# Token-major u, v and q in groups of 512 weight columns, one bank per token tile, row tiles outermost

## The chip, the cores and the metric

The kernel runs on one core of one Trainium2 chip. The metric is the device time of one execution in microseconds: the median of three runs. A profiled execution, taken separately, gives the trace.

## What is computed

Two layers of a hybrid backbone over 512 latent tokens (x) and 256 context tokens (ctx), 1024 features, all in fp32. A layer begins with

```python
hx = modulate(rms_norm(x, norm1_g[l]), sx1, cx1)
hc = modulate(rms_norm(ctx, norm1_g[l]), sc1, cc1)
zx = split_in(hx @ w_in[l])   # a, b (conv) | q | k | v | u, v (gating) | 3 gates
```

and the parts of that product feed a convolution module (width 31, with a layer norm), a windowed attention with 8 query and 2 key heads, and a spatial gating unit (`gelu(u) * (sgu_w @ layer_norm(gelu(v)))`). Three gated projections are summed, projected and added to x; a gated MLP with a width-3 convolution follows. Layer 0 computes all this for x and ctx, layer 1 for x alone (and k, v of ctx).

## The kernel before, in words

Every product is exact to about fp32: activations and weights are split into a hi and a lo half, and three matmuls (hi hi, lo hi, hi lo) are accumulated. Weights come in raw tiles of 1 MB (tag `raw`, two buffers, SyncE's queue); `hilo` makes two halves of half a raw tile (one copy on ScalarE, line 114, one subtraction on VectorE, line 117; tag `hl`). Pairs of halves alternate between two pools: two pairs in `wp` and, from the spatial gating to the end of q, one pair in the pool of the gating stage.

Most products are feature-major (`linear_steps`): a weight tile of 128 columns is stationary, 512 x tokens or 256 ctx tokens move. Those of u, v, q and of k, v are token-major (`token_group`): 128 tokens are stationary, 256 weight columns move. A group of 256 columns is done one token tile after the other, 8 row tiles x 3 matmuls each; two token tiles share a bank. u, v and q have 512 columns each, so two groups; layer 0 has six token tiles (four of x, two of ctx), layer 1 four. Evacuations are a gelu on ScalarE (`uv_group`) or a copy (q).

PSUM has eight banks: tag `S` is one buffer of two banks, `b` has three, `x` two, `c` one. `acc_ps(0)` gives a bank for x, `acc_ps(1)` for ctx; where `wide[0]` is set, the first goes round x, x, b, b, b and the second round S, c, by a counter that only grows. `wide[0]` is set from the convolution's products to the end of u, and in the MLP, and not set for q.

The order of the code in a layer: convolution products a, b (`ab`); v, u, with background steps (`tick`: convolution taps on VectorE) between; gates of branch 0 with the spatial gating (`sgu`) in the background; k, v product (line 757); norm and rotation of k, its transposes (line 793, tag S); `drain` of the background; `conv_ln`, the layer norm of the convolution, with a mean matmul (line 570, tag S), and for x and for ctx the sums of squares (line 400, tag b) and their broadcast (line 413, tag b); q (line 807); two early gates of branch 2; then the projections of the convolution (tag cy as operand) and of the gating as filling between the steps of the attention.

Within that, instructions are planned by a list scheduler: each engine takes the first one in priority (the order of the code, shifted for weights and evacuations) whose inputs and buffers are there in the scheduler's own timing, and executes that order as it stands.

At the start of the MLP (`up_first`) four products per part of 256 tokens follow the sums and the broadcast of the norm of the parts, with the same tags.

Of the kernel before, what the change touches and what calls it, by code (L numbers as in the profile page):

```python
# [12 lines left out]
AF = mybir.ActivationFunctionType  # L13
# [43 lines left out]
def layout(inputs):  # L57
    """the arrays of the launch: transposes and concatenations of the inputs, by tiles of 128 partitions"""
    v = {k: np.asarray(a) for k, a in inputs.items()}
# [20 lines left out]
def body(tc, I, out):  # L80
# [19 lines left out]
    def acc_ps(c):  # L100
        """a bank for a product of x (0) or of ctx (1); where nothing else needs them, from the other tags too"""
        if not wide[0]:
            return c_ps() if c else x_ps()
        turns[c] += 1
        if c:
            return (c_ps, s_ps)[turns[1] % 2]()
        return (x_ps, x_ps, b_ps, b_ps, b_ps)[turns[0] % 5]()
# [27 lines left out]
    def newton(src, n, scale, tag):  # L135
        """1/sqrt(src*scale + EPS) of a [128, n] operand"""
        v = T(cp, [128, n], F32, "nv" + tag[0], 1)
        ts(v, src, float(scale), mul, EPS, add)
        t = T(cp, [128, n], I32, "nt" + tag[0], 1)
        ts(t, v.bitcast(I32), 1, ALU.logical_shift_right)  # L140
        y = T(cp, [128, n], I32, "ny" + tag, 1)
        ts(y, t, -1.0, mul, float(0x5F3759DF), add)
        ts(v, v, -0.5, mul)
        u = T(cp, [128, n], F32, "nu" + tag[0], 1)
        yf = y.bitcast(F32)
        for _ in range(3):
            tt(u, yf, yf, mul)
            tt(u, u, v, mul)
            stt(yf, u, 1.5, yf, add, mul)
        return yf  # L150

# [1 line left out]
    def evac():  # L153
# [55 lines left out]

# [1 line left out]
    msk = T(sp, [128, NT], F32, "t", NTP)[:, :512]  # L211
# [12 lines left out]

    # feature vectors of both layers, one column per 128 features
    def load_fv(l):
# [6 lines left out]
    def load_ff(l, pool):  # L233
        """taps and biases of the MLP's convolution, one column per 128 features"""
        ff = T(pool, [128, FF_N], F32, "ff", 1)
        nc.scalar.dma_start(out=ff, in_=I["ff"][l])
        return ff
# [41 lines left out]
    def load_cond():  # L279
        """silu(c), silu(c_ctx): hi and lo parts as columns, and rows in DRAM"""  # L280
        st = T(xp_, [128, 16], F32, "st", 1)
# [13 lines left out]
    def ada_start():  # L295
        """shift and scale of the first norm, both conditions; those of the first four feature tiles come first"""
        for g2 in range(2):
# [29 lines left out]
    def ada(l, pool, blocks, both):  # L327
        """modulations of 128 features each, by rows of the transposed matrix; of c_ctx too for those in both"""
        for h in range(2):
# [17 lines left out]

# [1 line left out]
    bgs = []  # L349
# [24 lines left out]
    def paced(r):  # L374
        """in the schedule, not before the products traced so far"""
        if last[0] is not None:
            tc.add_manual_dep(r.ins, last[0].ins.name, SCHED)

# [1 line left out]
    def segs_of(full):  # L380
# [14 lines left out]
    def rstd_diag(acc, o, n, scale):  # L395
        """1/sqrt of the feature sums of acc[:, o:o+n], by token tiles on the diagonals of [128, 128] blocks"""
        nt = n // 128
# [9 lines left out]
    def bcast_diag(dg, n, bp=None):  # L407
        """the diagonals on every partition"""
        if bp is None:
# [14 lines left out]
    def norm_mod(xs, bp, hs, o, n, a, sh):  # L424
        """hi and lo pages of x * bp * a + sh"""
        v = slice(o, o + n)
# [11 lines left out]
    def linear_steps(res, w, cs, hs, segs, k0=0):  # L438
        """feature-major product of one 128-column tile, w hi/lo [128, k, cols]: per segment (psum, offset, length, segment);
        yields the time that the tensor engine has been given"""  # L440
        nk = w[0].shape[1]
# [16 lines left out]
    def token_group(hs, c0, nt):  # L458
        """token-major product of a group of 256 columns: (psum [128, 2, 256], first of its two token tiles)"""
        raw = load8(I["w_in"][l], c0)  # L460
# [15 lines left out]

    def tg_parts(p, t0, ng):
        """parts of a pair of token tiles that lie in one tile of ng: (psum, group, index, count)"""
        if t0 // ng == (t0 + 1) // ng:
            return [(p, t0 // ng, t0 % ng, 2)]  # L480
        return [(p[:, a:a + 1], (t0 + a) // ng, (t0 + a) % ng, 1) for a in range(2)]

    def tr(o, i):
        nc.tensor.transpose(o, i, ident)

# [1 line left out]
    def load_x(gap=None):  # L487
# [32 lines left out]
    for l in range(2):  # L520
# [15 lines left out]

# [1 line left out]
        wide[0] = True  # L538
# [92 lines left out]

# [1 line left out]
        EVP[0] = 150  # L633
# [12 lines left out]

        def uv_group(dst, c0, c):
            for p, t0 in token_group(hs, c0 + c * 256, nt):
                for q, g, a, n in tg_parts(p, t0, ng):
                    with evac():  # L650
                        act(out=dst[g][:, a:a + n, c * 256:c * 256 + 256], in_=q, func=AF.Gelu_apprx_tanh)

        U = [page("g2", 4, n=1536).rearrange("p (t d) -> p t d", t=3) for _ in tg]
        Vv = [page("g2", 4, n=1536).rearrange("p (t d) -> p t d", t=3) for _ in tg]
        for c in range(2):
            uv_group(Vv, 2304, c)
            tick(11)

# [48 lines left out]
        ys = []  # L707
        for c in range(2):
            uv_group(U, 1792, c)
            tick(11)  # L710
        wide[0] = False

# [1 line left out]
        def gate_steps(b, j, dst):  # L714
# [14 lines left out]
        def gated_steps(dst, w, j, ys, ao=False):  # L729
            """projection of a branch, times (tanh + 1) of its gate in place: twice the sigmoid's share"""  # L730
            if j % 4 == 0:
# [20 lines left out]

# [1 line left out]
        vt = page("g2", 4, F32R, 1536)  # L754
# [8 lines left out]
        def head_norm(pg, tmp, ss):  # L763
            """sums of squares by head of pg [128, tiles, heads, 64]"""
            act(out=tmp, in_=pg.rearrange("p t h d -> p (t h) d"), func=AF.Square)
            V.tensor_reduce(out=ss, in_=tmp, axis=AX.X, op=add)

        def head_rot(pg, nh, tb, t0, n, sw, rs):
            """pg [128, n tiles, nh heads, 64] in place: scale by head, gain, rotation of the x tiles"""
            fl = pg.rearrange("p t h d -> p (t h) d")  # L770
# [34 lines left out]

# [1 line left out]
        Q = [T(sp, [128, 1536], F32, "g2", 4).rearrange("p (t i k d) -> p t i k d", t=3, i=4, k=2) for _ in tg]  # L807
        for g in range(2):
            for p, t0 in token_group(hs, 1024 + g * 256, nt):
                for q, gr, a, n in tg_parts(p, t0, ng):  # L810
                    with evac():
                        acopy(Q[gr][:, a:a + n, :, g, :], q.rearrange("p t (i d) -> p t i d", i=4))
        rings.pop()
# [25 lines left out]
        def fill(us):  # L839
            """dense products for that many microseconds of the tensor engine, in front of what is emitted next"""  # L840
            credit[0] = min(credit[0], 0) + us
# [7 lines left out]

        # pairs of heads of one token tile  # L850
        ssq = T(cp, [128, 48], F32, "ssq", 1)
# [32 lines left out]
        def keys_of(t):  # L884
            """key tiles, their runs in psum (offset, length, first key), offset of the mask"""
            if t < 3:
# [7 lines left out]
        def scores(pr, i):  # L894
            """probabilities of one head"""
            t, kv, i0, (qd, ql) = pr["t"], pr["kv"], pr["i0"], pr["q"]
# [23 lines left out]
        def turn_P(pr, g):  # L920
            """hi and lo parts of the transposed probabilities of two key tiles"""
            kk = keys_of(pr["t"])[0][g * 2:g * 2 + 2]
# [104 lines left out]
        wide[0] = True  # L1027
# [1 line left out]
        if l == 0:  # L1029
# [51 lines left out]

# [1 line left out]
        if l == 0:  # L1083
# [36 lines left out]
        def up_first(due):  # L1120
            """two pairs of tiles part by part, behind the norm of each part"""
            ws = [up_load(j) for j in range(2)]
# [96 lines left out]
```

## Time and profile before

| what | value |
|---|---|
| median of 3 runs | 2134.9 us (2134.14 to 2138.05) |
| profiled execution, span | 2133.2 us |
| TensorE matmul busy | 2098.5 us (98%) |
| weight loads (beside matmuls) | 1801.1 us (84%) |
| VectorE busy | 1569.4 us (74%) |
| ScalarE busy | 895.9 us (42%) |
| mean DMA rate | 99 GB/s |

A matmul's duration in the trace is from its start to its modelled end, and the next one starts before that, so what a matmul costs is the distance of starts. Groups below are named by line (L446), engine, operation and output tile <- input tiles, then the shapes.

### The profile page before, as it was taken

How to read it: one execution, taken by the hardware profiler on the slowest of the kernel's cores; microseconds unless marked ns; L12 is line 12 of the kernel's file. 1: busy time of each engine (PE TensorE's matmuls, PEld its weight loads, DVE VectorE, ACT ScalarE, POOL GpSimd, SP SyncE). 2: the span in 40 equal slices, each digit the busy share in tenths (PEclk: the TensorE clock that was granted, in tenths of full speed). 3: DMA queues.
4: the chain of work that ended last, by engine and by line, in shares of the span. 5: the costliest groups of instructions: out<-in, count | busy, mean ns of one | idle time of the engine just before them, and what ended most of it. 6: DMA issues, size and time to landing. Idle time of an engine off the chain costs nothing.

```text
span 2133.2 us, 30441 instructions
## 1 busy us (share of the span) xinstructions
PE 2098.5 (98%) x12108; PEld 1801.1 (84%) x12108; DVE 1569.4 (74%) x3134; ACT 895.9 (42%) x1489; POOL 0.2 (0%) x4
## 2 busy tenths in 40 slices
PE   6999999999999999999999999999999999999999
PEld 2899898877888998888888898979777888888887
DVE  6679887888757778867595767998877367655554
ACT  6522235567623453323231334434577336333331
POOL 0000000000000000000000000000000000000000
PEclk8999999999999999999999999999999999999999
DMA  8122112212245223444243423222111333232321
GB/s 274 60 76 66 53 60 80 89 50 80 79 111 184 76 83 135 141 137 148 99 149 103 164 75 105 88 76 80 60 40 60 91 129 99 94 104 79 119 91 67
DMA packets 158805, 210.94 MB, mean 99 GB/s; under 512 B 6724, under 2 KB 109892, under 8 KB 158664
## 3 DMA queue, kind: packets, MB, share of 16 engines
q1 hardware_dynamic: 154048, 202.40, 28.7%
q10 hardware_dynamic: 4616, 6.61, 1.0%
q8 instruction: 95, 1.56, 0.3%
q14 instruction: 46, 0.38, 0.1%
HBM read 204.78 MB, written 4.20 MB: 98 GB/s over the span
## 4 chain that ended last, share of the span: by engine, by line
PE 81%; DVE 11%; DMA 3%; ACT 3%; issue 1%; SPq 0%; DVEq 0%; ACTq 0%
PE x L446 10%; PE x L448 10%; PE x L447 10%; PE b L447 8%; PE b L446 8%; PE b L448 8%; DVE cy L120 4%; PE c L446 3%; PE c L447 3%; PE c L448 3%; PE S L907 2%; DVE hl L117 2%; PE b L944 2%; PE b L927 2%; PE S L446 2%; PE S L447 2%
## 5 line engine op out<-in xcount | busy, mean ns | idle before, releaser
L114 ACT ACTIVATE hl<-raw 128x1024 fp32r<-128x1024 f32 x264 | 279.0, 1059 | 487.3 <-PE c L447 199.0
L117 DVE TENSOR_TENSOR hl<-raw,hl 128x1024 fp32r<-128x1024 f32 x264 | 322.4, 1223 | 193.7 <-ACT hl L114 190.8
L446 PE MATMUL x<-h,hl 128*128 128x512 f32 (+1 forms) x760 | 294.3, 389 | 7.0 <-ACT h L114 7.0
L448 PE MATMUL x<-h,hl 128*128 128x512 f32 (+1 forms) x760 | 292.0, 385 | 1.6 <-DVE hl L117 1.6
L447 PE MATMUL x<-h,hl 128*128 128x512 f32 (+1 forms) x760 | 293.0, 386 | 0.0
L120 DVE SCALAR_TENSOR_TENSOR cy<-cy,fv 128x497 f32<-128x497 f32 (+29 forms) x240 | 208.3, 881 | 2.9
L447 PE MATMUL b<-h,hl 128*128 128x512 f32 (+1 forms) x552 | 203.6, 370 | 0.0
L446 PE MATMUL b<-h,hl 128*128 128x512 f32 (+1 forms) x552 | 203.5, 370 | 0.0
L448 PE MATMUL b<-h,hl 128*128 128x512 f32 (+1 forms) x552 | 202.9, 368 | 0.3 <-DVE hl L117 0.3
L446 PEld LDWEIGHTS x<-h,hl 128*128 128x128 f32 x760 | 145.0, 192 | 33.7 <-ACT h L114 7.9
L448 PEld LDWEIGHTS x<-h,hl 128*128 128x128 f32 x760 | 145.0, 191 | 28.7 <-DVE hl L117 2.7
L447 PEld LDWEIGHTS x<-h,hl 128*128 128x128 f32 x760 | 145.1, 191 | 24.2 <-DVE h L117 0.2
L448 PEld LDWEIGHTS b<-h,hl 128*128 128x128 f32 x552 | 103.9, 188 | 18.0 <-DVE hl L117 0.7
L446 PEld LDWEIGHTS b<-h,hl 128*128 128x128 f32 x552 | 103.9, 189 | 17.0
L447 PEld LDWEIGHTS b<-h,hl 128*128 128x128 f32 x552 | 104.0, 189 | 16.4
L446 PE MATMUL c<-h,hl 128*128 128x256 f32 x400 | 112.7, 282 | 0.1
L448 PE MATMUL c<-h,hl 128*128 128x256 f32 x400 | 112.7, 282 | 0.0
L447 PE MATMUL c<-h,hl 128*128 128x256 f32 x400 | 112.6, 281 | 0.1
L120 DVE SCALAR_TENSOR_TENSOR m<-b,ff,m 128x511 f32<-128x511 f32 (+2 forms) x118 | 80.9, 688 | 36.5 <-ACT m L1092 35.0
L339 DVE CUSTOM_DVE_ANT_0 t<-t,srow,adab 128x512 f32<-128x512 f32 (+1 forms) x128 | 92.4, 745 | 4.5 <-DMA t<-in_adat 4.2
L339 DVE CUSTOM_DVE_ANT_0 t<-t,srow,mod 128x512 f32<-128x512 f32 (+1 forms) x128 | 91.7, 746 | 1.8 <-DMA t<-in_adat 0.9
L114 ACT ACTIVATE PT<-b 128x512 fp32r<-128x512 f32 (+2 forms) x128 | 62.3, 500 | 58.6 <-PE b L944 39.6
(322 smaller groups left out, 5124.5 us busy)
## 6 DMA issues: line engine op xcount, KB each, us to landing
raw<-in_w_in SPq DMA_DIRECT2D x44, 1024.0 KB, 5.1
raw<-in_ffn_up SPq DMA_DIRECT2D x44, 1024.0 KB, 5.1
t<-in_adat SPq DMA_DIRECT2D x160, 256.0 KB, 3.0
raw<-in_ffn_down SPq DMA_DIRECT2D x22, 1024.0 KB, 4.9
raw<-in_w_o SPq DMA_DIRECT2D x8, 1024.0 KB, 7.1
g<-in_xt SPq DMA_DIRECT2D x8, 768.0 KB, 5.7
m<-in_ada SPq DMA_DIRECT2D x16, 256.0 KB, 5.4
h<-in_ada SPq DMA_DIRECT2D x16, 256.0 KB, 5.4
```

Of the source, the lines that this page charges most:

```text
L114: act(out=o, in_=i, func=AF.Copy)
L117: V.tensor_tensor(out=o, in0=a, in1=b, op=op)
L120: return V.scalar_tensor_tensor(out=o, in0=a, scalar=s, in1=b, op0=op0, op1=op1)
L339: paced(V.tensor_tensor_reduce(out=w[:, 512:].bitcast(BF16) if c else w[:, :512], in0=w[:, :512], in1=sr[:, c], scale=1.0, scalar=o if h e ...
L446: nc.tensor.matmul(p, w[0][:, k, cs], hi[:, o:o + n], start=(k == 0), stop=False)
L447: nc.tensor.matmul(p, w[0][:, k, cs], lo[:, o:o + n], start=False, stop=False)
L448: last[0] = nc.tensor.matmul(p, w[1][:, k, cs], hi[:, o:o + n], start=False, stop=(k == nk - 1))
L907: nc.tensor.matmul(sp_[:, o:o + n], ql[r, c], KT[kv][r, ko:ko + n], start=False, stop=True)
L927: r_ = nc.tensor.transpose(pt[:, a * 256 + i * 128:a * 256 + i * 128 + 128], pr["P"][i][:, (g * 2 + a) * 128:(g * 2 + a) * 128 + 128], ident)
L944: r_ = nc.tensor.matmul(po[:, :256], vs, half[:, a * 256:a * 256 + 256], start=fi and i == 0, stop=la and i == 1)
```

## The change

`token_wide` takes the place of `token_group` for u, v and q (k, v keep it). It takes one bank of 512 columns per token tile, all at once, and goes over the weights in four passes of two row tiles; in a pass every token tile gets its 6 matmuls of 512 columns. A raw load is now 512 rows by 512 columns, and `hilo` splits two row tiles by 512 columns. Evacuations are one per token tile, after the last pass. Of the 22 background steps of u or v 5 come after each of the first three passes and 7 at the end (before, 11 after each group). For q `wide[0]` is set. Docstrings and comments go too; they change nothing.

```diff
+    def token_wide(hs, c0, nt, between=None):
+        ps_ = [acc_ps(t >= 4)[:, :512] for t in range(nt)]
+        for q in range(4):
+            if q % 2 == 0:
+                raw = load4(I["w_in"][l], q * 256, c0).rearrange("p (k c) -> p k c", k=4)
+            w = hilo(raw[:, q % 2 * 2:q % 2 * 2 + 2, :], 2)
+            for t in range(nt):
+                for k in range(2):
+                    hi, lo = hs[q * 2 + k]
+                    c = slice(t * 128, t * 128 + 128)
+                    nc.tensor.matmul(ps_[t], hi[:, c], w[0][:, k, :], start=(q + k == 0), stop=False)
+                    nc.tensor.matmul(ps_[t], lo[:, c], w[0][:, k, :], start=False, stop=False)
+                    last[0] = nc.tensor.matmul(ps_[t], hi[:, c], w[1][:, k, :], start=False, stop=(q * 2 + k == 7))
+            if between and q < 3:
+                between()
+        return ps_
...
-        def uv_group(dst, c0, c):
-            for p, t0 in token_group(hs, c0 + c * 256, nt):
-                for q, g, a, n in tg_parts(p, t0, ng):
-                    with evac():
-                        act(out=dst[g][:, a:a + n, c * 256:c * 256 + 256], in_=q, func=AF.Gelu_apprx_tanh)
+        def uv_group(dst, c0):
+            for t, p in enumerate(token_wide(hs, c0, nt, lambda: tick(5))):
+                with evac():
+                    act(out=dst[t // ng][:, t % ng, :], in_=p, func=AF.Gelu_apprx_tanh)
+            tick(7)
...
-        for c in range(2):
-            uv_group(Vv, 2304, c)
-            tick(11)
+        uv_group(Vv, 2304)
...
-        for c in range(2):
-            uv_group(U, 1792, c)
-            tick(11)
+        uv_group(U, 1792)
...
-        for g in range(2):
-            for p, t0 in token_group(hs, 1024 + g * 256, nt):
-                for q, gr, a, n in tg_parts(p, t0, ng):
-                    with evac():
-                        acopy(Q[gr][:, a:a + n, :, g, :], q.rearrange("p t (i d) -> p t i d", i=4))
+        wide[0] = True
+        for t, p in enumerate(token_wide(hs, 1024, nt)):
+            with evac():
+                acopy(Q[t // ng][:, t % ng].rearrange("p i k d -> p k i d"), p.rearrange("p (k i d) -> p k i d", k=2, i=4))
+        wide[0] = False
```

## Rows read from the trace of the kernel before

**Rows 1.** The page, part 1: busy time, share of the span and instructions of each engine.
```profile
PE 2098.5 (98%) x12108; PEld 1801.1 (84%) x12108; DVE 1569.4 (74%) x3134; ACT 895.9 (42%) x1489; POOL 0.2 (0%) x4
```

**Rows 2.** Timeline of TensorE, layer 0's v: start us, us, what; 48 starts apart.
```profile
121.38 0.28 PE L471 MATMUL x<-hl,h 128*128 128x256 f32 x1
...
127.14 0.28 PE L471 MATMUL b<-hl,h 128*128 128x256 f32 x1
```

**Rows 3.** Timeline of TensorE, gates of layer 0, 512 columns; 15 starts apart.
```profile
241.21 0.39 PE L446 MATMUL x<-h,hl 128*128 128x512 f32 x1
...
244.61 0.39 PE L446 MATMUL x<-h,hl 128*128 128x512 f32 x1
```

**Rows 4.** Busy time by stretch: v, u of layer 0; v, u, then gates of layer 1.
```profile
core 0: us, PE busy (x) PEld busy (x) DVE busy (x) ACT busy (x) POOL busy (x), PEclk, DMA share, GB/s
121.00:191.00 70.00, 69.95 (x580) 69.52 (x579) 61.09 (x87) 19.20 (x29) 0.00 (x0) 1.00 0.15 46
...
1334.00:1382.00 48.00, 47.32 (x388) 46.84 (x387) 45.99 (x95) 21.97 (x34) 0.00 (x0) 1.00 0.27 89
1382.00:1439.00 57.00, 54.44 (x261) 44.47 (x260) 56.12 (x91) 17.86 (x25) 0.00 (x0) 0.97 0.23 74
```

**Rows 5.** Timeline of TensorE, layer 0, from q's first matmul to the convolution's projection.
```profile
284.80 0.28 PE L471 MATMUL x<-hl,h 128*128 128x256 f32 x1
...
296.13 0.88 PE L484 MATMUL S<-identr,t 128*128 128x128 f32 x6 [0.20 <-DVE t L117]
...
300.90 1.53 PE L570 MATMUL S<-t,ones 128*128 128x512 f32 x4
...
321.69 0.60 PE L413 MATMUL b<-t,ones 128*128 128x256 f32 x2
...
325.23 0.40 PE L446 MATMUL x<-h,hl 128*128 128x512 f32 x1
...
341.90 0.39 PE L446 MATMUL x<-cy,hl 128*128 128x512 f32 x1
```

**Rows 6.** Timeline of VectorE: last readers of mean and broadcast, last convolution operand.
```profile
307.21 0.42 DVE L120 SCALAR_TENSOR_TENSOR cy<-S,cy 128x256 f32<-128x256 f32 x1
...
324.86 1.01 DVE L117 TENSOR_TENSOR t<-cy,b 128x512 f32<-128x512 f32 x2
...
333.16 0.96 DVE L117 TENSOR_TENSOR cy<-t,cy 128x768 fp32r<-128x768 f32 x1
```

**Rows 7.** Timeline of layer 1's same stage, TensorE, and the broadcast's last reader on VectorE.
```profile
1456.35 0.28 PE L471 MATMUL x<-hl,h 128*128 128x256 f32 x1
...
1482.70 1.12 PE L413 MATMUL b<-t,ones 128*128 128x512 f32 x2 [0.19 <-DVE t L117]
...
1484.13 0.40 PE L446 MATMUL x<-h,hl 128*128 128x512 f32 x1
...
1495.06 0.40 PE L446 MATMUL x<-cy,hl 128*128 128x512 f32 x1
...
1488.62 0.68 DVE L117 TENSOR_TENSOR t<-cy,b 128x512 f32<-128x512 f32 x1
```

**Rows 8.** The page, part 5: weight splits (busy us, mean ns, idle before).
```profile
L114 ACT ACTIVATE hl<-raw 128x1024 fp32r<-128x1024 f32 x264 | 279.0, 1059 | 487.3 <-PE c L447 199.0
L117 DVE TENSOR_TENSOR hl<-raw,hl 128x1024 fp32r<-128x1024 f32 x264 | 322.4, 1223 | 193.7 <-ACT hl L114 190.8
```

**Rows 9.** Timeline of TensorE, start of the MLP in layer 0.
```profile
730.30 0.28 PE L448 MATMUL x<-h,hl 128*128 128x256 f32 x1
732.61 0.70 PE L413 MATMUL b<-t,ones 128*128 128x256 f32 x2 [2.02 <-DVE t L117]
734.95 0.58 PE L446 MATMUL x<-h,hl 128*128 128x256 f32 x1 [1.65 <-ACT h L114]
...
741.93 0.50 PE L400 MATMUL b<-ones,t 128*128 128x1 f32 x4
742.29 0.36 PE L446 MATMUL b<-h,hl 128*128 128x256 f32 x1
```

**Rows 10.** Busy time and granted clock (PEclk) in the stretch after that idle time.
```profile
735.00:740.00 5.00, 5.00 (x23) 5.00 (x24) 4.25 (x12) 4.55 (x11) 0.00 (x0) 0.50 0.01 2
```

More of the change, by code (lines that the diff above doesn't have):

```diff
@@ L475, in token_group @@
         return res
[L477 to L481, printed above, removed]
+    def token_wide(hs, c0, nt, between=None):
[14 more added lines that the diff above has]
+        return ps_
     def tr(o, i):
```

## The prediction

> **What bounds the kernel now.** I read the busy table first: TensorE is occupied 98% of the span [rows 1], so the question is how densely it is fed. Start to start in the timeline, the 48 matmuls of 256 columns of one v tile take 5.76 us, 120 ns each [rows 2], and 15 matmuls of 512 columns take 3.40 us, 226.7 ns each [rows 3]. Then the table by stretch: in layer 0's v and u products TensorE has no hole (69.95 of 70 us) while VectorE has 9 us to spare; in layer 1 the same stage and the gate products behind it leave VectorE 2.0 us of 48 and 0.9 us of 57 [rows 4]. So layer 0's v and u are bound by TensorE's cadence, layer 1's by VectorE (31 convolution taps a channel tile, weight splits, gating). Last I read the stage from the k, v product to the convolution's projection, where two things run side by side: q's matmuls, and the chain k transposes, mean, deviation sums, broadcasts, on which the projection depends [rows 5 to 7]. There q is what keeps TensorE busy while that chain waits for VectorE and ScalarE.
>
> **Part 1, fewer and longer matmuls.** u, v and q take 3 products x 6 token tiles x 8 row tiles x 3 passes x 2 halves = 864 matmuls of 256 columns in layer 0 and 576 in layer 1; after the change 432 and 288 of 512. One long one for two short ones saves 240 - 226.7 = 13.3 ns [rows 2, 3]: 5.7 us in layer 0 (v and u 3.8, q 1.9) and 3.8 us in layer 1 (v and u 2.6, q 1.3), 9.6 us at most. Layer 0's v and u should keep their 3.8 us; in layer 1 I take 0.5 of 2.6, since VectorE has nothing to give there [rows 4] (bounds 0 and 2.6). q's share is inside part 3.
> The Trainium skill ("TensorE: Matmul & The Clock Gate", section "Back-to-back issue gap") gives columns / 2.4 GHz plus 2.5 ns for a gap; by that estimate a pair would save 2.5 ns, and all of them 1.8 us. The rows show a fixed part of some 13 ns per matmul, and the rows decide.
>
> **Part 2, weights.** A pass over two row tiles now uses one pair of halves: 36 matmuls x 226.7 = 8.2 us in layer 0, 24 x 226.7 = 5.4 us in layer 1. The next pair costs 1.06 us on ScalarE and 1.22 us on VectorE [rows 8], and three pairs are in the rings, so loading and splitting hide behind a pass. If the cover goes (the fourth pair shares a buffer with the second and waits for its last user), a split is bare: 2.3 us. The count of splits, 1 MB loads, background steps (44 a layer) and evacuated columns doesn't change; fewer, wider evacuations cost nothing, ScalarE being idle most of the stage [rows 4].
> The Trainium skill (same page, section "Loop structure matters more than you think") speaks against row tiles outermost: it wants all row tiles of one output before the next, lest TensorE wait for a transfer between matmuls. A split of 2.3 us against a pass of 5.4 us gives no such wait here; what the new order does cost is the next part.
>
> **Part 3, banks.** With row tiles outermost every token tile needs its bank until the last pass. v, u and q each want six banks at once in layer 0 (four of x and b, then S and c), four in layer 1. Counting the rotation of acc_ps through the code: layer 0's q gets b, x, x, b for tiles 0 to 3, S for 4, c for 5; layer 1's q gets b, b, b, x. In the code q stands behind the convolution's norm, which itself takes S (mean), then b four times (sums and broadcast of x, sums and broadcast of ctx; twice in layer 1).
> So the question is in which order tiles of one tag get their banks, by the code or by who is ready first. The start of the MLP in layer 0 answers it. After the first product's (x) last matmul, at 730.30, TensorE stands idle for 2.02 and 1.65 us with the same activations ready for the second product, which is tagged b; it starts only at 742.29, 0.36 us after the sums of the last part (line 400, b, earlier in the code) have run at 741.93 [rows 9]. b has three banks, and only the broadcast of 732.61 holds one. So a tag's banks are handed out in the order of the code, even to something not ready.
> Applied to layer 0: from q's start at 284.80 tiles 1, 2 and 5 can run passes 0 to 2: 9 x 6 matmuls = 12.3 us, to 297. Pass 3 needs the pair that passes 1 of all tiles release. Tile 4 (S) must wait for the mean of 300.90 and its last reader at 307.63: 18 matmuls, 4.1 us, inside the chain's waits. Tile 0 (b) waits for the ctx broadcast, 321.69; tile 3 for the x broadcast's last reader, about 325.5 [rows 5, 6]. Without the two splits that now delay the chain's VectorE steps I put these 1.5 us earlier or less: 320.2 and 325.0. Tile 0 to 324.3, tile 3 to 329.1 (pass 1 done at 327.7, plus split 2.6, so pass 3 can start at 330.3), pass 3 36 x 226.7 = 8.2 us, to 338.5, where q now ends at 325.23. The two early gates follow, 16.7 us as now (325.23 to 341.90), so the projection starts at 355.2 in place of 341.90: +13.3 us, q's own saving included. The early gates can't move forward: they want x and c, held by tiles 1, 2 and 5, and the weight ring.
> Layer 1: tile 3 (x) runs 4.1 us from 1456.35. Tiles 0 and 1 wait for the broadcast at 1482.70, tile 2 for its last reader at 1489.30 [rows 7]. 54 matmuls from 1483.4 end at 1495.7, pass 3 (5.4 us) at 1501.2 against 1484.13 now; gates 10.9 us; projection at 1512.1 against 1495.06: 17.0, less 1.5 for the lighter chain: +15.5 us.
> Clock: after the idle 730.58 to 734.95 the granted clock stood at 0.50, the 1.2 GHz level, and 23 matmuls of 256 columns took 5.0 us or more where they take 2.8 [rows 9, 10]. Both q stages get longer idle stretches than that; I add 2.5 us each, 5 together (bounds 0 and 7).
> Layer 1's v has one b tile behind the broadcast of the ctx norm, but two x tiles give 8 us of work meanwhile: nothing. The rotation's phase shifts by four behind q: the second product of the MLP's start gets an x bank and fills part of that 3.7 us hole: -2.5 us (bounds -5 and +2, since other products get b instead).
>
> **Sum**: -3.8 - 0.5 + 13.3 + 15.5 + 5 - 2.5 = +27.0 us on the profiled execution, whose span is 2133.2 us; the median of the runs lies 1.7 us above it. 2134.9 + 27 = 2162 us.
>
> **Rivals.** (a) Banks go to whoever is ready first. Then tile 4 of layer 0's q takes S at about 290, before the k transposes of 296.13 are ready, and holds it to the end of q at 284.8 + 32.7; the transposes slip by 21 us, and the convolution's last operand, done at 334.12, comes at 351 to 355 instead of well before 341.9 [rows 5, 6]: +9 to +13, less 3.8, 0.5 and layer 1's 1.3, plus some clock: 2139 to 2143. For it: the change needs only one such case. Against it: rows 9.
> (b) Faster: TensorE's idle time is filled. What is needed is 12 to 20 us of products that use neither b nor S and come behind q in the code; the gates of the third branch are such (16.7 and 10.9 us in front of the projection, more behind). If their banks and weight halves come free early, q's end and the gates only change places, the projection starts as now, and the cadence decides: 2134.9 - 6 to - 9.6 = 2125 to 2129. It decides from the point at which an early gate gets a pair of halves before tile 0 has run. Against it: if the ring keeps the code's order as the banks do, no gate gets halves before q's fourth pass.
> (c) The change does not do what it says: 512-column token products run no closer than pairs of 256, and banks never bind: 2134 to 2136. Against it: rows 2 and 3 differ in nothing but the columns.
>
> **How the numbers follow.** Likeliest 0.76, own range 2146 to 2178 (lower: chain 4 us shorter in each layer, no clock cost, gain of the phase 5; upper: no lighter chain, clock 7 each, nothing kept of v and u). (a) 0.08, (b) 0.12, (c) 0.04. The range goes down to 2131 to take in (a) and (c), and leaves (b) out: 2131 to 2178. A measurement of this kernel tells 0.2%, 4.3 us, from no change: faster 0.12; same 0.07 ((c) and the lower part of (a)); slower 0.81.
>
> **What would show it.** Right: TensorE holes of 5 to 10 us between q's first tiles and the two broadcasts in both layers, a granted clock under 1 there, q's b tiles starting right behind line 413, projection 13 and 15 us later after the k, v product; v and u of layer 0 at 227 ns a matmul and 3.8 us shorter. Wrong: q dense from its first matmul (b or c), k transposes behind q (a), or early gates between q's tiles (b).

## The result, and the profile after

| | before | after |
|---|---|---|
| median | 2135.1 us (2134.14 to 2138.05, 4 runs) | 2165.42 us (2163.2 to 2165.69, 4 runs) |
| ratio to before | | 1.0135, 95% interval 1.0122 to 1.0147 |
| profiled execution, span | 2133.2 us | 2163.5 us |
| mean granted clock | 0.994 | 0.982 |

The change costs 30.3 us, in the medians as in the spans; 27 were forecast. The busy table says as little as the one before the change [rows 1]: TensorE has 720 matmuls fewer and 5 us more of busy time, in a span that is 30 us longer.

```profile
PE 2103.6 (97%) x11388; PEld 1773.9 (82%) x11388; DVE 1570.8 (73%) x3134; ACT 897.7 (41%) x1483; POOL 0.2 (0%) x4
```

**Where the 30 us are.** The execution is cut into six stages at starts of TensorE's matmuls that both kernels have: the first matmul of layer 0's v, of its k, v product and of the convolution's projection, then the same three in layer 1, and the last matmul of all. Every later table row is read in this way. Times are in microseconds.

| stage | before | after | difference |
|---|---|---|---|
| A: v of layer 0 to its k, v product | 146.14 | 141.36 | -4.78 |
| B: k, v product to projection, layer 0 | 74.38 | 89.33 | +14.95 |
| C: projection to v of layer 1 | 992.67 | 989.56 | -3.11 |
| D: v of layer 1 to its k, v product | 104.41 | 104.01 | -0.40 |
| E: k, v product to projection, layer 1 | 56.07 | 76.76 | +20.69 |
| F: projection of layer 1 to the last matmul | 634.02 | 635.98 | +1.96 |

Ahead of A lie 121.38 and 122.30 us. (That start, which the change doesn't touch, lay between 120.98 and 126.02 in the profiled executions below, so stages are compared, not ends.) Stage F lies between 634.02 and 640.00 in all these executions; the phase of the rotation explains a part of that (see the last experiment), and the rest stays open.

Stage A first. This is TensorE's timeline of v and u in layer 0, the first and the last of 288 matmuls, to be set beside [rows 2] (a line gives start us, us, engine, line, operation, output tile <- inputs, shapes):

```profile
122.30 0.40 PE L488 MATMUL x<-hl,h 128*128 128x512 f32 x1
...
187.38 0.39 PE L490 MATMUL c<-hl,h 128*128 128x512 f32 x1
```

65.08 us over 287 distances are 226.8 ns each, the value of [rows 3], without a hole. The busy times by stretch follow: v and u of layer 0, v and u of layer 1, then layer 1's gates (columns as in [rows 4]):

```profile
122.30:192.00 69.70, 69.70 (x310) 57.73 (x309) 66.08 (x91) 19.04 (x24) 0.00 (x0) 1.00 0.15 47
...
1342.55:1387.08 44.53, 44.23 (x196) 36.34 (x194) 44.26 (x89) 22.23 (x35) 0.00 (x0) 1.00 0.30 95
1387.08:1443.00 55.92, 54.69 (x242) 45.31 (x241) 52.45 (x90) 17.74 (x24) 0.00 (x0) 0.88 0.24 76
```

Stage B is TensorE in layer 0 from q's first matmul on, to be set beside [rows 5]. A bracket gives the idle time ahead of an instruction and who ended it:

```profile
280.94 0.40 PE L488 MATMUL x<-hl,h 128*128 128x512 f32 x1
...
292.27 0.87 PE L496 MATMUL S<-identr,t 128*128 128x128 f32 x6 [0.26 <-DVE t L117]
...
297.04 2.19 PE L582 MATMUL S<-t,ones 128*128 128x512 f32 x4 [2.50 <-DVE g L117]
303.12 0.79 PE L488 MATMUL S<-hl,h 128*128 128x512 f32 x1 [3.90 <-DVE cy L120]
...
312.34 1.02 PE L413 MATMUL b<-t,ones 128*128 128x512 f32 x2
...
317.86 0.83 PE L413 MATMUL b<-t,ones 128*128 128x256 f32 x2 [4.17 <-DVE t L117]
318.18 0.94 PE L488 MATMUL b<-hl,h 128*128 128x512 f32 x1
...
336.34 0.39 PE L446 MATMUL x<-h,hl 128*128 128x512 f32 x1
...
352.99 0.39 PE L446 MATMUL x<-cy,hl 128*128 128x512 f32 x1
```

Three of the six token tiles start without a wait. Tile 4, on S, starts when the mean's last reader (line 120) frees S. The tiles on b begin 0.32 us behind the last broadcast, line 413. Then come pass 3, the early gates and the projection. Stage E is the same in layer 1, to be set beside [rows 7]:

```profile
1464.00 0.40 PE L488 MATMUL x<-hl,h 128*128 128x512 f32 x1
...
1468.65 0.40 PE L490 MATMUL x<-hl,h 128*128 128x512 f32 x1
1474.71 1.54 PE L496 MATMUL S<-identr,t 128*128 128x128 f32 x6 [5.67 <-DVE t L117]
1480.05 2.05 PE L582 MATMUL S<-t,ones 128*128 128x512 f32 x2 [3.80 <-DVE g L117]
1486.86 1.87 PE L400 MATMUL b<-ones,t 128*128 128x1 f32 x8 [4.76 <-DVE t L117]
1491.88 2.07 PE L413 MATMUL b<-t,ones 128*128 128x512 f32 x2 [3.15 <-DVE t L117]
1492.97 1.42 PE L488 MATMUL b<-hl,h 128*128 128x512 f32 x1
...
1512.44 0.39 PE L446 MATMUL x<-h,hl 128*128 128x512 f32 x1
...
1523.32 0.40 PE L446 MATMUL x<-cy,hl 128*128 128x512 f32 x1
```

The one tile on x gets its 18 matmuls. Then come four holes, 17.4 us together, between which TensorE has nothing but the transposes of k and the norm's own steps, and then all the rest of q behind the broadcast. The granted clock in the two q stages was 0.88 and 0.80 (PEclk, third from the end):

```profile
280.94:352.99 72.05, 61.16 (x268) 49.11 (x267) 54.35 (x135) 32.16 (x55) 0.00 (x0) 0.88 0.18 59
...
1464.00:1523.32 59.32, 41.50 (x164) 31.75 (x163) 40.01 (x95) 24.14 (x40) 0.00 (x0) 0.80 0.16 53
```

Last comes the start of the MLP in layer 0, to be set beside [rows 9]: there is one hole of 2.47 us where there were two of 2.02 and 1.65, and from 744 to 749 us the granted clock was 0.93, where it had stood at 0.50 behind the two holes [rows 10].

```profile
740.70 0.70 PE L413 MATMUL b<-t,ones 128*128 128x256 f32 x2
...
746.93 0.36 PE L446 MATMUL x<-h,hl 128*128 128x256 f32 x1 [2.47 <-DVE edge L1145]
...
750.70 0.56 PE L446 MATMUL b<-h,hl 128*128 128x256 f32 x1
```

### The profile page after: what moved, and what is told of

Same layout as the page of the kernel before. It is cut to its first block, busy times and chain, and to the rows that moved or that the text cites. A ratio compares the mean times of both kernels' runs of the same rounds, so it can differ in the third digit from the quotient of the medians.

```text
span 2163.5 us, 28995 instructions
## 1 busy us (share of the span) xinstructions
PE 2103.6 (97%) x11388; PEld 1773.9 (82%) x11388; DVE 1570.8 (73%) x3134; ACT 897.7 (41%) x1483; POOL 0.2 (0%) x4
## 4 chain that ended last, share of the span: by engine, by line
PE 86%; DVE 9%; ACT 2%; DMA 2%; issue 1%; SPq 0%; ACTq 0%; DVEq 0%
PE x L446 11%; PE x L447 11%; PE x L448 11%; PE b L447 8%; PE b L446 8%; PE b L448 8%; PE c L446 3%; PE c L448 3%; PE c L447 3%; DVE cy L120 3%; PE S L915 2%; PE b L952 2%; PE S L447 2%; PE S L446 2%; PE S L448 2%; PE b L935 2%
## 5 line engine op out<-in xcount | busy, mean ns | idle before, releaser
L120 DVE SCALAR_TENSOR_TENSOR cy<-cy,fv 128x503 f32<-128x503 f32 (+29 forms) x240 | 208.5, 880 | 3.0
L448 PEld LDWEIGHTS b<-h,hl 128*128 128x128 f32 x552 | 104.1, 189 | 17.4
L446 PE MATMUL b<-y,hl 128*128 128x512 f32 (+1 forms) x260 | 89.0, 342 | 0.2 <-DVE g L120 0.2
```

Source lines behind the costliest of these rows:

```text
L120: return V.scalar_tensor_tensor(out=o, in0=a, scalar=s, in1=b, op0=op0, op1=op1)
L446: nc.tensor.matmul(p, w[0][:, k, cs], hi[:, o:o + n], start=(k == 0), stop=False)
L448: last[0] = nc.tensor.matmul(p, w[1][:, k, cs], hi[:, o:o + n], start=False, stop=(k == nk - 1))
```

## The experiments

All are edits of the kernel after. Ratios are to the kernel before, run beside it on the same chip, where it took 2135.5 to 2137.2 us; the stages are in microseconds.

| kernel | median | ratio, 95% interval | A | B | C | D | E | F |
|---|---|---|---|---|---|---|---|---|
| u, v alone (e1_vu) | 2128.2 | 0.9962 (0.9950 to 0.9975) | 141.35 | 74.37 | 992.50 | 100.34 | 56.06 | 634.79 |
| q alone (e2_q) | 2173.97 | 1.0173 (1.0158 to 1.0188) | 146.15 | 91.76 | 988.43 | 103.15 | 76.41 | 637.25 |
| q ahead of the norm (e3_q_ahead) | 2153.91 | 1.0080 (1.0066 to 1.0094) | 141.44 | 84.15 | 993.99 | 102.60 | 64.07 | 640.00 |
| mixed by layer (e7_mix) | 2139.41 | 1.0014 (1.0003 to 1.0024) | 141.39 | 74.40 | 993.20 | 101.45 | 64.02 | 636.17 |
| banks x, x, c, b (e4_xxcb) | 2153.53 | 1.0076 (1.0062 to 1.0090) | 141.35 | 89.38 | 990.53 | 102.77 | 67.74 | 634.96 |
| filled holes (e6_fill) | 2159.82 | 1.0104 (1.0090 to 1.0119) | 141.34 | 89.41 | 991.09 | 100.34 | 72.64 | 635.23 |
| phase of before (e5_phase) | 2160.87 | 1.0112 (1.0095 to 1.0129) | 141.35 | 89.76 | 991.91 | 101.15 | 72.76 | 634.16 |
| own banks, one slip (e8_own_banks) | 2154.54 | 1.0079 (1.0065 to 1.0093) | 141.36 | 94.86 | 988.31 | 102.68 | 60.48 | 638.46 |
| own banks (e9_own_all) | 2134.02 | 0.9988 (0.9979 to 0.9998) | 141.37 | 72.68 | 990.14 | 102.77 | 60.47 | 638.48 |
| and q's norms later (e10_norms_later) | 2128.14 | 0.9961 (0.9949 to 0.9974) | 141.39 | 72.73 | 990.25 | 102.70 | 55.33 | 636.89 |
| and layer 1's phase (e11_phase_l1) | 2124.21 | 0.9939 (0.9926 to 0.9953) | 141.29 | 72.77 | 990.28 | 101.29 | 55.27 | 635.38 |

### Which part gains, which part loses

u and v alone are made in the new form; q goes back to groups of 256.

```diff
-        wide[0] = True
-        for t, p in enumerate(token_wide(hs, 1024, nt)):
-            with evac():
-                acopy(...)
-        wide[0] = False
+        for g in range(2):
+            for p, t0 in token_group(hs, 1024 + g * 256, nt):
+                ...
```

> Only u and v are made in groups of 512 columns; q stays in groups of 256, behind the convolution's norm. Theory (banks cost, cadence gains): q's stage is again dense in both layers, the rotation's phase is that of before, and what is left is the cadence of u and v: 3.8 us in layer 0 (288 pairs of 13.3 ns) and about 0.5 us in layer 1, 2130.6 us, 0.998 of before. In the trace, 227 ns a matmul in layer 0's v, k and v product some 3.8 to 4.8 us earlier after v's start, layer 1's gates giving back most of what u and v gain there. Rival, row tiles outermost cost by themselves (weights, banks of v and u): 2135 us or more. Rival, layer 1's 2.6 us are kept too: 2128.5 us.

This kernel is faster than before by 0.38%, 8.1 us in the medians, more than the 4.3 expected. A gives 4.8 us as expected, B and E are those of before (74.37, 56.06). The surprise is D: it is 4.07 us shorter, where I had said that VectorE would keep all but 0.5. Stage D by stretch, in the kernel before, in the kernel after, in this one and in e6_fill (further below):

```profile
1334.58:1438.99 104.41, 101.17 (x643) 90.83 (x642) 101.52 (x183) 39.82 (x59) 0.00 (x0) 0.98 0.25 81
```

```profile
1342.55:1446.56 104.01, 102.48 (x451) 84.60 (x450) 100.20 (x182) 40.27 (x59) 0.00 (x0) 0.93 0.26 81
```

```profile
1329.26:1429.60 100.34, 98.27 (x452) 80.40 (x450) 99.40 (x180) 40.16 (x59) 0.00 (x0) 0.98 0.26 84
```

```profile
1342.85:1443.19 100.34, 98.30 (x452) 80.39 (x450) 99.35 (x180) 40.28 (x59) 0.00 (x0) 0.98 0.27 84
```

VectorE was nearly full, and the stage still became 4 us shorter: VectorE's idle time fell from 2.9 to 0.9 us, and its busy time from 101.52 to 99.40, three instructions fewer, so 2.1 us of its work no longer fell into the stage. The full change has the same u and v, but a lower clock: 0.93 of 2.4 GHz over 104.01 us is 7.3 us of clock not granted, against 2.0 here. e6_fill, whose code up to there is that of the full change, kept 0.98 and 100.34 us. The kernel before varies too: e2_q below, which has its u and v, took 103.15 us at a granted clock of 1.00. So a gain of D of 2.8 to 4.1 us is real, and the clock gave it back in one execution and not in another. What decides that was not found; in the full change the low clock stood in the gates behind u (0.88 from 1387.08 to 1443.00).

q alone is made in the new form; u and v go back.

```diff
-        uv_group(Vv, 2304)
+        for c in range(2):
+            uv_group(Vv, 2304, c)
+            tick(11)
... (U likewise)
```

> Only q is made in groups of 512 columns; u and v stay in groups of 256. Theory: the whole loss is here, and more than the loss of the full change, since the gain of u and v is missing: 2165.4 + 4.3 = 2169.7 us, 1.0163 of before; idle stretches of TensorE of 4 to 6 us between q's first tiles and the broadcasts in both layers. Rival, u and v have a part in the loss (their banks, or the splits that come later): 2150 to 2162 us.

The median is 2173.97 us, and the interval 1.0158 to 1.0188 holds the 1.0163 expected. q in its new form makes the whole loss (B +17.4, E +20.3), and u and v have no part in it. That it does so by its banks is for the next experiments. B is 2.4 us longer than in the full change, which was not followed up.

### Is it the order of the code that hands out the banks

q's lines are moved ahead of the convolution's norm, nothing else.

```diff
+        Q = [...]
+        wide[0] = True
+        for t, p in enumerate(token_wide(hs, 1024, nt)):
+            ...
         cv = []
         for _ in conv_ln(cv):
             pass
-        Q = [...]
-        wide[0] = True
-        ...
```

> The full change, with q's six lines of code moved ahead of the convolution's norm; nothing is added or left out. Theory (a tag's banks are handed out in the order of the code): in layer 1 q takes no S bank and gets its b banks before the norm's sums, so it runs dense from its first matmul, the norm's chain follows beside it and beside the gates, and the stage from q's start to the convolution's projection is 37 to 39 us as before in place of 59. In layer 0 the norm's mean now waits for S, held by q's tile 4 until q ends: q from 281 to about 314.5, mean at 315 in place of 300.9, the chain's 20.8 us to the last broadcast and 12.4 us to the last operand bring the projection to 348, 6 us behind before. Sum: -4.3 + 6 - 1.3 - 2.5 = -2, 2133 us (2129 to 2142). Rival (banks go to whoever is ready first, so that the place in the code changes nothing): 2165 us.

The median is 2153.91 us, and both numbers missed it. The theory's main point held and the rival's fell: the place in the code alone takes 12.7 us off E, and q runs dense from its first matmul in both layers (in layer 1, 96 matmuls without a wait for a bank). But I had expected the norm to run beside q. Behind q in the code, the norm's matmuls also stand behind q's on TensorE, and start when q ends. TensorE in layer 1 in this kernel, the mean (line 588 here), the broadcast and the projection:

```profile
1486.78 1.02 PE L588 MATMUL S<-t,ones 128*128 128x512 f32 x2
...
1499.51 1.02 PE L413 MATMUL b<-t,ones 128*128 128x512 f32 x2
1510.31 0.80 PE L446 MATMUL x<-cy,hl 128*128 128x512 f32 x1 [9.78 <-ACT t L737]
```

In the kernel before, the mean is line 570:

```profile
1472.64 1.07 PE L570 MATMUL S<-t,ones 128*128 128x512 f32 x2
```

The mean comes 40.5 us behind the first matmul of the k, v product, where it came 33.7 before (1472.64 against 1438.99); these 6.9 us are most of the 8.0 by which E is longer than before. From the mean to the projection the chain needs 23.5 us, the early gates cover 11 of them, and TensorE then waits 9.78.

The next kernel is mixed by layer: u and v are wide (in groups of 512), q is as before in layer 0, and wide and ahead of the norm in layer 1.

> u and v in groups of 512 columns in both layers, q in groups of 256 behind the convolution's norm in layer 0 as before, q in groups of 512 columns ahead of the convolution's norm in layer 1. Theory: the gain of u and v (4.3 us) and q's own cadence in layer 1 (1.3 us), with no bank waited for: 2129.3 us, 0.9974 of before, and TensorE dense in both q stages. Rival (512-column q costs by its banks wherever it stands): layer 1's q stage 5 to 20 us longer, 2136 to 2150 us.

The median is 2139.41 us, on the rival's side. B is that of before, E is 64.02 as in the run above, 8 us longer than before. So the order of q and the norm in the code has a price both ways.

### Fewer shared banks

In layer 1 the norm uses neither the c bank nor the two x banks. Here q takes these three and one b bank.

```diff
-        ps_ = [acc_ps(t >= 4)[:, :512] for t in range(nt)]
+        ps_ = [(x_ps, x_ps, c_ps, b_ps)[t]()[:, :512] if l and c0 == 1024 else acc_ps(t >= 4)[:, :512] for t in range(nt)]
```

> The full change, except that layer 1's q takes the banks x, x, c, b for its four token tiles in place of b, b, b, x. Theory: three tiles in place of one can run passes 0 to 2 ahead of the norm's broadcasts, 36 more matmuls of 226.7 ns or 8.2 us that no longer follow behind the broadcast, and less of the stage at the lower clock: 2165.4 - 8 to 10 = 2156.5 us. Rival (something else than the b banks holds layer 1's q, the weight halves or the norm's chain): within 2 us of 2165.4.

E falls by 9.0 us, as worked out from 36 matmuls more ahead of the broadcast: in the trace three tiles, 54 matmuls, now run there and one follows. The ratio fell from 1.0135 to 1.0076, 12.6 us; D and F give 1.2 and 1.0 of the rest.

Then q and the norm were to have no bank in common. The norm's sums and broadcasts go to one S tile, q's tile 4 to b.

```diff
-            bps = [bcast_rstd(acc, o, n, 1.0 / 512) for o, n, c in segs]
+            sb = s_ps()
+            bps = [bcast_diag(rstd_diag(acc, o, n, 1.0 / 512, sb[:, 768 + o // 4:896 + o // 4]), n, sb[:, o:o + n]) for o, n, c in segs]
...
+        ps_ = [b_ps() if t == 4 and c0 == 1024 else acc_ps(t >= 4)[:, :512] for t in range(nt)]
+        turns[1] += l == 0 and c0 == 1024
```

> The full change with q where it is, behind the convolution's norm; only the banks differ: the norm takes its deviation sums and both broadcasts in one S tile (S is free from the mean on) and q's tile 4 takes a b bank, so that q and the norm share no bank. The tiles, the matmuls and the order of the code are those of the full change. Theory (the loss is the shared banks): q runs dense beside the norm's chain, which keeps its place ahead of q: stage from q's start to the convolution's projection 57.1 - 1.9 = 55.2 us in layer 0 (72.05 in the full change) and 38.7 - 1.3 = 37.4 us in layer 1 (59.3), granted clock 1.0 in both. Sum: 2165.4 - 16.9 - 21.9 = 2126.6 us (2123 to 2131), 0.9955 of before, 1 to 3 us below the version with u and v alone. Rival (weight halves of 512 columns, or the passes themselves, hold q up): idle stretches stay between q's tiles, 2140 to 2165 us.

The median is 2154.54 us, and layer 0 doesn't test the theory, since the edit had a slip. Its last line moves the rotation on only after tile 5 has been given its bank, so tile 5 took S, which the norm now keeps to its last reader. B became the longest of all, 94.86 us. TensorE in layer 0, then VectorE's last reader of the S tile:

```profile
314.89 1.22 PE L414 MATMUL S<-t,ones 128*128 128x256 f32 x2 [2.88 <-DVE t L117]
327.13 0.77 PE L496 MATMUL S<-hl,h 128*128 128x512 f32 x1 [11.02 <-DVE t L117]
```

```profile
326.57 0.41 DVE L117 TENSOR_TENSOR t<-cy,S 128x256 f32<-128x256 f32 x1
```

One bank of six stops all of q for 11.02 us. In layer 1, where the edit did what it should, q runs dense, and E is 60.48 us: 16.3 us less than in the full change, yet 4.4 more than before. VectorE between the norm's sums and its broadcast shows why (line 783 is the reduction of q's head norms in this kernel):

```profile
1492.91 0.16 DVE L120 SCALAR_TENSOR_TENSOR nyt<-nut,nyt 128x4 f32<-128x4 f32 x1
1493.02 0.69 DVE L783 TENSOR_REDUCE ssq<-PT 128x8 f32<-128x512 f32 x1
1493.62 0.15 DVE L117 TENSOR_TENSOR nut<-nyt 128x4 f32<-128x4 f32 x1
1493.69 0.68 DVE L783 TENSOR_REDUCE ssq<-PT 128x8 f32<-128x512 f32 x1
1494.28 0.15 DVE L117 TENSOR_TENSOR nut<-nut,nvt 128x4 f32<-128x4 f32 x1
...
1495.62 0.68 DVE L117 TENSOR_TENSOR t<-identr,nyt 128x512 f32<-128x512 f32 x1
```

A wide q is done for all its tiles at nearly the same time. Its head norms (0.68 us each) are then ready at once and fall between the small steps of the norm's inverse root. From the sums to the broadcast are 6.06 us on TensorE, here (1490.29 to 1496.35), against 4.22 before (1478.48 to 1482.70 [rows 7]). The sums and the broadcast here, then the sums before:

```profile
1490.29 0.97 PE L401 MATMUL S<-ones,t 128*128 128x1 f32 x8
1496.35 1.12 PE L414 MATMUL S<-t,ones 128*128 128x512 f32 x2
```

```profile
1478.48 1.05 PE L400 MATMUL b<-ones,t 128*128 128x1 f32 x8
```

The next kernel mends the slip: tiles 4 and 5 of q take b and c outright.

```diff
+        ps_ = [(b_ps, c_ps)[t - 4]() if t >= 4 and c0 == 1024 else acc_ps(t >= 4)[:, :512] for t in range(nt)]
... (the norm's S tile as above)
```

> As the version in which q and the norm were to share no bank (e8_own_banks), but now in layer 0 too: there q's tile 5 still took the S bank, since the rotation stood one step off; here tile 4 takes b and tile 5 takes c. Theory (shared banks hold layer 0's q): from the k, v product to the projection 74 to 76 us in layer 0 (74.4 before, 89.3 in the full change, 94.9 in e8_own_banks), no idle stretch of 11 us ahead of the last broadcast's readers, clock 1.0 throughout; layer 1 as in e8_own_banks, 60.5 us against 56.1 before. Sum: 2154.5 - 19.5 = 2135 us (2131 to 2139). Rival (passes and weight halves hold layer 0's q by themselves): 2145 us or more.

The median is 2134.02 us, 1.0 below the central value. B is 72.68 us, 1.7 below before and 1.3 below the stretch named, and E is 60.47 as foretold. No matmul of v, u or q waits in this kernel. Taking the shared banks away takes back the whole loss of 30 us, though E and F are still 4.4 and 4.5 us longer than before.

In the next kernel q's head norms are also ordered behind the early gates (`paced` gives the planner an order and adds no wait on the chip):

```diff
-        def head_norm(pg, tmp, ss):
+        def head_norm(pg, tmp, ss, pace=False):
...
-            act(out=tmp, in_=pg.rearrange("p t h d -> p (t h) d"), func=AF.Square)
+            r_ = act(out=tmp, in_=pg.rearrange("p t h d -> p (t h) d"), func=AF.Square)
+            if pace:
+                paced(r_)
... (the call for q passes True)
```

> As e9_own_all, and the squares of q's head norms are ordered behind the two early gates' products in the planner's order (an ordering alone, no wait on the chip), so that they don't come into the convolution's norm. Theory (in layer 1 the wide q is done for all its tiles at once, and its head norms, 2.7 us of reductions and more of small steps, fall into the norm's chain on VectorE, between its sums and its broadcast and behind it): layer 1 from the k, v product to the projection 57 us in place of 60.5, layer 0 unchanged or 1 us shorter: 2131 us. Rival (the chain is longer for another reason, such as the weight splits or the evacuations): layer 1 stays at 60 us or more, 2135 us.

E is 55.33 us, 5.1 less and 0.7 below before, where the theory had 57; the median is 2128.14, below the 2131 expected. VectorE at the same place, then TensorE's projection:

```profile
1473.21 0.16 DVE L120 SCALAR_TENSOR_TENSOR nyt<-nut,nyt 128x4 f32<-128x4 f32 x1
1473.41 0.16 DVE L117 TENSOR_TENSOR nut<-nyt 128x4 f32<-128x4 f32 x1
1473.60 0.16 DVE L117 TENSOR_TENSOR nut<-nut,nvt 128x4 f32<-128x4 f32 x1
1473.80 0.16 DVE L120 SCALAR_TENSOR_TENSOR nyt<-nut,nyt 128x4 f32<-128x4 f32 x1
1474.00 0.69 DVE L117 TENSOR_TENSOR t<-identr,nyt 128x512 f32<-128x512 f32 x1
```

```profile
1484.75 0.50 PE L447 MATMUL x<-cy,hl 128*128 128x512 f32 x1 [0.44 <-ACT t L740]
```

No head norm is left in the chain, and the 5.76 us for which the projection waited in e8_own_banks and e9_own_all are 0.44.

### What the holes cost by the clock

78 matmuls whose result nobody reads are put into layer 1's holes.

```diff
+        if l:
+            pd = c_ps()[:, :512]
+            for i in range(78):
+                last[0] = nc.tensor.matmul(pd, hs[i % 8][0][:, :128], wg[0][0], start=True, stop=True)
```

> The full change, plus 78 products of 128x512 in layer 1 that nobody reads, into the bank c, which is free there, behind q in the code; they run where TensorE has nothing else, in the holes of layer 1's q stage. Theory (the holes cost time twice, as waits and by the clock of 1.2 GHz behind them): the granted clock stays at 1.0 through the stage, the norm's matmuls take 0.9 to 1.1 us a step again in place of 1.5 to 2.1, and q's first b tile runs at 227 ns: 3 to 4 us less in the stage, 2161.9 us (0.9984 of the full change), although TensorE does 17 us more work. Rival (the clock costs nothing, the chain waits for VectorE alone): 2165 us or a little more, since the added products can stand in front of a ready one.

E falls by 4.1 us, though TensorE does more. The q stage by stretch (it begins at 1460.59), then the broadcast and the first b tile:

```profile
1461.50:1515.83 54.33, 53.78 (x238) 42.81 (x236) 39.31 (x95) 23.22 (x40) 0.00 (x0) 1.00 0.18 59
```

```profile
1486.05 1.13 PE L413 MATMUL b<-t,ones 128*128 128x512 f32 x2
1486.62 0.79 PE L494 MATMUL b<-hl,h 128*128 128x512 f32 x1
```

The granted clock is 1.00 in place of 0.80, and the broadcast takes 1.13 us in place of 2.07. Of the 20.7 us that E lost, some 4.1 are therefore clock and 16.6 are waiting. (The ratio fell by 0.0031, 6.6 us, since D came out shorter too.)

### The phase of the rotation

The wide q takes four turns of the rotation x, x, b, b, b in each layer, so all products behind it get other banks than before. One turn more, behind q in both layers, undoes that shift.

```diff
+        turns[0] += 1
```

> The full change, with the rotation of banks advanced by one behind q in both layers, so that all products behind q get the banks that they have before the change. Theory (the phase gained 2.5 us at the MLP's start): the holes of 2.0 and 1.7 us between layer 0's first two MLP products come back in place of one of 2.5 us, and the time is 2165.4 + 2.5 = 2168 us. Rival (the phase gives nothing, or other products lose as much): 2163 to 2166 us.

C grew by 2.35 us, where 2.5 were expected, and the holes at the MLP's start are 2.03 and 1.65 again, so that term holds. The total went the other way, to 2160.87, for a reason I had overlooked: the same count gives layer 1's q two x banks in place of one, 36 matmuls run ahead of the broadcast in place of 18, and E falls by 4.0 us. D (shorter by 2.9) and F (by 1.8) add to it.

The last kernel is e10_norms_later with `turns[0] += 2` behind layer 1's q alone:

> As e10_norms_later, with the rotation of banks advanced by two behind layer 1's q, so that layer 1's output projection and MLP get the banks of before, while layer 0's keep the phase that saved 2.3 us at the MLP's start. Theory (the phase costs layer 1's end what it saves in layer 0): from layer 1's projection to the end 634.5 us, as in the kernels with the phase of before (634.0, 634.8, 634.2), in place of 636.9: 2126 us, 0.995 of before. Rival (what layer 1's end lost has nothing to do with the banks): 636 to 637 us, 2128 us.

The median is 2124.21 us, 0.6% below before and the best version here. F gave 1.5 of the 2.4 us expected; another 1.4 came in D, whose length differs from execution to execution, so the phase's share of the 3.9 us in the medians is at most 1.5.

## Why the prediction was right, step by step

**What bounds the kernel.** "Layer 0's v and u are bound by TensorE's cadence" held: A is 4.8 us shorter, forecast 3.8. "Layer 1's by VectorE" was wrong: stage D gives 4.07 us at an equal clock (e1_vu), or 2.8 against e2_q, where 0.5 was forecast with 2.6 as the upper bound. VectorE was busy for 45.99 of 48 us [rows 4], but 2.0 us of the gain came out of its idle time in the whole stage, and 2.1 from work that no longer fell into the stage. A full engine is a bound only if somebody waits for all of its work. That the full change shows 0.40 us in D, close to my 0.5, is luck: the clock took the rest.

**Part 1.** A matmul took 226.8 ns, as read off [rows 3]. The saved distances are 3.8 us, as forecast. v and u became 4.4 us shorter (69.75 to 65.31), since in the kernel before they held short gaps as well, the longest distance being 330 ns. The estimate worked out from the Trainium skill's formula for an isolated matmul's gap ("TensorE: Matmul & The Clock Gate", "Back-to-back issue gap"), 1.8 us for all of u, v and q, does not agree with this case: layer 0's v and u alone gave 4.4.

**Part 2.** This held. Splits hide in v and u (they have no hole), and in layer 1's q stage of the full change the only wait for a half is 0.43 us. The bare split ahead of pass 3 in layer 0 (forecast 1.2 us of idle time, from a split priced at 2.6 us there and at 2.3 in part 2) did not come: the matmuls from 318.18 to 336.34 follow each other without a hole. e9_own_all and e10_norms_later, with row tiles outermost, run v, u and q without any such wait. The loop order that the Trainium skill shows as good ("TensorE: Matmul & The Clock Gate", "Loop structure matters more than you think") finishes one output's row tiles before the next, and the loop that it shows as bad waits for a transfer ahead of every matmul. These two kernels have the other order and no such wait; what the order cost here was banks.

**Part 3.** The rule, that a tag's banks go out in the order of the code, was read from one place [rows 9]. The full change bears it out: q's b tiles stood behind the norm's broadcasts, although layer 1's x tile already ran with the same weights at 1464.00 and TensorE had 17.4 us of holes. e3_q_ahead confirms it (move the lines, and the wait goes), and e9_own_all shows the price (with no bank in common the 30 us are taken back). e8_own_banks shows something else, that one bank held to its last reader stops the whole loop (11 us).
Layer 0 went as written: tiles 1, 2 and 5 ran first, tile 4 behind the mean's reader, tile 0 behind the ctx broadcast, tile 3 behind the other (321.80; forecast 325.0, with q starting 3.9 us later), then pass 3 and the gates. The forecast was 13.3 and 2.5 for the clock, 15.8; measured are 14.95. In part that is luck, since two errors offset each other: the chain was not 1.5 us earlier (the ctx broadcast came 36.92 us behind q's start, 36.89 before), and the bare split of 1.2 us was not there.
In layer 1 the forecast was 15.5 and 2.5, 18; measured are 20.69. At full clock it is 16.6 (e6_fill), so waiting was 1.1 over, and the clock, 4.1 for 2.5, is the mis-sized term. Part of the 1.1 is the credit of 1.5 for a lighter chain. From q's start to line 413 it takes 26.35 us before and 25.46 in e6_fill, so it is 0.9 lighter at full clock. In the full change it took 27.88, with the granted clock at 0.50 from 1471.95 to 1495.84.
Of the signs named ahead, "holes of 5 to 10 us" came as more and smaller ones: 2.50, 3.90 and 4.17 in layer 0, and 5.67, 3.80, 4.76 and 3.15 in layer 1.

**Phase.** The forecast was -2.5; C shows -3.1, and e5_phase undoes 2.35 of it. The +2 in F was not in the sum.

**Sum.** -4.78 + 14.95 - 3.11 - 0.40 + 20.69 + 1.96 and 0.92 ahead of A make +30.2; the forecast was +27.0.

**Rivals.** (a) First ready: refuted by the full change itself (k's transposes ran at 292.27, tile 4 on S at 303.12) and by e3_q_ahead. (b) Filled by gates: refuted, as the early gates run behind q at 336.34 and 1512.44. (c) Nothing happens: refuted by e1_vu and e2_q. What no rival contained is what e3_q_ahead and e9_own_all showed: with the banks out of the way, the norm's place behind q, or q's own norms on VectorE, become the next thing to wait for.

## What to carry to other kernels

A loop order that holds one accumulation bank per output tile until the last pass is paid for at its neighbours. List the tags of all that runs beside it, in the order of the code, before counting the matmuls saved. One shared bank was enough to stop the whole loop here (11.02 us), and giving the neighbour its own was worth more (ratio 0.9988) than moving either in the code (1.0080). A loop that finishes all its outputs at once also makes all their followers ready at once; keep these out of the chain that is late (5.1 us here).

## Not expected of the hardware

The holes cost twice, and the second cost was larger than forecast (4.1 us for 2.5). In the full change's layer 1 the granted clock stood at 0.50, the 1.2 GHz level, in this stretch, in which TensorE had little but waits:

```profile
1471.95:1495.84 23.89, 9.41 (x23) 5.92 (x24) 14.21 (x32) 5.16 (x8) 0.00 (x0) 0.50 0.00 1
```

The broadcast took 2.07 us in it, against 1.12 before [rows 7]; filling the holes with useless products shortened the stage by 4.1 us. And stage D came out between 100.34 us (granted clock 0.98) and 104.01 us (0.93) with the same code up to its end (e6_fill and the full change), so that a difference of 3 us in one profiled execution can be the clock alone.
